# Attention steps moved into the value stage, low products turned, and the input sum one block earlier, in a one-core decoder block

## The chip, the core and the metric

The kernel runs on one core of a Trainium2 chip. The metric is device time in microseconds (us) of one execution, smaller is better. A core has a tensor engine (PE) that multiplies a loaded 128x128 block of weights with a moving matrix, a vector engine (DVE), a scalar engine (ACT), and queues through which DMA engines move data. Each engine works through its own instruction list in the order in which the kernel writes it; engines wait for one another by semaphores.

## The reference, cut to what matters

One layer of a hybrid decoder block, 256 tokens (T) by 2048 channels, all in 32-bit floats:

```
u    = rmsnorm(h, g_mix_pre)
q,k,v of 12 dilated-window heads and of 4 stick-breaking heads, and two gates = split(u @ w_in)
ya   = dilated window softmax attention (3 groups of 4 heads), groups mixed per head slot
yb   = stick-breaking attention (4 heads)
h   += rmsnorm((sigmoid(gate_a) * (ya @ w_branch_a) + sigmoid(gate_b) * (yb @ w_branch_b)) @ w_out)
h   += rmsnorm((gelu(conv(gate_ff)) * conv(value)) @ w_down)      # up projection and causal conv of width 3
h   += sigmoid(h @ w_ple_gate) * (p @ w_ple_in)
```

A head slot s (0 to 3) holds one head of each of the three window groups and one stick-breaking head. A window head needs scores q.k with a bias, a softmax over them, and the probabilities times v. The stick-breaking head needs z = q.k, l = softplus of z masked, cumulative sums of l by products with triangular ones, exp, and the result times v.

## The kernel before, in words

**Precision by splitting.** A product of two 32-bit operands is made of three products of rounded parts: high times high, high times low, low times high. Of each weight tile of 128x1024 (eight blocks of 128x128) ACT makes the rounded high part (`high`, L153) and DVE the rest (`low`, L156). The activations lie as high part (256 columns) and low part (256 columns) side by side. `mul` (L227) multiplies one block: a 512-column matmul of the high weights with both parts (L232), and a 256-column one of the low weights with the high part (L234). With `turned` the 256-column matmul goes first (L231). `mul1` and `mul_first` use three matmuls of 256 columns instead.

**Tiles and ticks.** Weight tiles come by DMA from the SP queue into five raw buffers and are split into seven pairs of high and low buffers. Every eight blocks PE reaches a new tile, and `block` calls `tick` (L181), which writes into the lists of ACT and DVE what is due: first deferred work, then the high parts of tiles some way ahead, then low parts. `defer` queues work in stages; each tick takes one new entry and runs the next stage of each entry under way (`due`, L165). Where more than two entries are waiting, the DVE part of deferred work stands before the low parts of that tick, else after them. The lookahead grows after the opening up to six tiles.

**The opening.** Seven columns (q of heads 0 to 3 and k of heads 0 to 2 of slot 0) are accumulated together, k block by k block (16 blocks), while the input arrives. At k = 14 the loop calls `flush` and `halves` (L370: the sum of squares of the input is split into two halves, DVE, ACT, DVE), at k = 15 `total` (L378: two matmuls with ones, then `rstd`, L358: the factor R on ACT and DVE). Column 7 (k of head 3) follows. The columns are taken out of PSUM by `qk_evac` (L469) in two stages: ACT copies one half of the bank, DVE adds (L286) and multiplies with R (L475); then the split into high (ACT, L484) and low (DVE, L482). Columns 0 and 1 are taken out at once, columns 2 to 7 by the ticks, one new column each: the first stage of column 2 at the first tick of column 7, that of column 6 at the third tick of the value stage.

**Slots.** For each slot come eight q and k columns (`("qk", s, c)`; slot 0 has them from the opening), then the value stage `v_units` (L507): 16 blocks kt, each with six 512-column matmuls (L517 to L519) into two banks; four weight blocks a kt, so a tick every second kt. Then the next slot's columns, and after slot 3 the gates.

**Attention steps.** `attention(s)` (L532) is a generator of eight steps; `att_step` (L624) runs one. In their order: e0 (scores of the first 128 queries, matmuls L550 on the q and k columns 0 to 2 and 4 to 6 in full precision, into the two-bank PSUM tile S; then bias, maximum, exp, sum, scaling on DVE and ACT, L556 to L560), e1 (the same for the other 128 queries, L530, on the split parts), z (L563 to L577: scores of the stick-breaking head, softplus, split), t0 and t1 (transposes of the probabilities into S, L588; copies out of it L589, L591), w (L594 to L605: cumulative sums into the PSUM tile z, exp, split), po and zo (L608 to L619: probabilities times v). S, z and po have one buffer each, so a step that writes S waits until the step before it that used S has been read out. Before, slot 0 runs two steps in its value stage, after kt = 11 and 15, the other slots four, after kt = 3, 7, 11 and 15; the rest follow one by one behind the columns of the next slot, or behind the gates. PE, DVE and ACT parts of a step stand in the engines' lists at that place.

Of the kernel before, what the change touches and what calls it, by code (L numbers as in the profile page):

```python
# [8 lines left out]
F32 = mybir.dt.float32  # L9
# [5 lines left out]
T = 256  # L15
# [18 lines left out]
LATE = 2  # L34
SETTLE = dict(even=8, turned=9)

TURNED = {("qk", 1, 1): 2, ("qk", 1, 4): 1, ("qk", 2, 1): 2, ("qk", 3, 2): 1, ("gb", 0): 2}


def _plan():  # L40
# [59 lines left out]
def hybrid_block_kernel(ctx: ExitStack, tc: tile.TileContext, gx, pT, convp, bias, masks, w, out):  # L100
# [9 lines left out]
    def f(ap):  # L110
        return ap.bitcast(F32)
# [137 lines left out]
    def mul1(ps, rhs, first, last):  # L249
# [3 lines left out]
        PE.matmul(ps, wh, rhs[:, T:], start=False, stop=False, skip_group_check=True)  # L253
        PE.matmul(ps, wl, rhs[:, :T], start=False, stop=last, skip_group_check=True)  # L254

    banks = {"of": [], "n": 0}

    def bank():
# [119 lines left out]
    def total(ps, sp):  # L378

        for n in range(2):  # L380
            PE.matmul(ps[:, :T], ones, sp[:, n * T:(n + 1) * T], start=n == 0, stop=n == 1)
        rstd(ps)
# [64 lines left out]
    for c, k, first, last in todo:  # L447
        if c == 0:
            if k == EARLY:
                at["grow"] = 0.5  # L450
                defer(*[squares2(h, (j, j + 2)) for j in range(0, KT, 4)])
            if EARLY - 2 <= k < KT - 2:
                usplit(u, k + 2, h[:, k + 2], gain(0, k + 2))
            if k == KT - 2:
                flush()
                sp = halves()
            if k == KT - 1:
                total(pat.tile([128, 2 * T], F32, name="z"), sp)
                DVE.tensor_scalar(Rq, R, 1.0 / math.sqrt(DH), None, op0=OP.mult)
        if first:  # L460
            mul_first(pss, c, u[:, k])
            c == 2 and filler(FILL)
            continue
        mul(pss[c], u[:, k], first, last)
    at["grow"] = 1
    nc.sync.dma_start(mk, masks)
    nc.sync.dma_start(cw, convp)
# [39 lines left out]
    def v_units(s):  # L507
        biases[s] = ab.tile([128, 1152], F32, name="bi")
        nc.sync.dma_start(biases[s], bias[s])
        pv = [bank() for _ in range(2)]  # L510
        assert next(plan)[0] == ("v", s)
        for kt in range(KT):
            wh, wl = block(4)
            for t in range(2):
                xh = u[:, kt, t * 128:(t + 1) * 128]
                xl = u[:, kt, T + t * 128:T + (t + 1) * 128]
                PE.matmul(pv[t], xh, wh, start=kt == 0, stop=False)  # L517
                PE.matmul(pv[t], xh, wl, start=False, stop=False)  # L518
                PE.matmul(pv[t], xl, wh, start=False, stop=kt == KT - 1)  # L519
            if kt % 4 == 3:  # L520
                yield
        V[s] = ab.tile([128, 2, 512], F32R, name="vs"), ab.tile([128, 512], F32, name="v")
        ACT.activation(V[s][0][:, 0], pv[0], AF.Copy, scale=Rc[:, 0:1])
        ACT.activation(V[s][1], pv[1], AF.Copy, scale=Rc[:, 1:2])
        DVE.scalar_tensor_tensor(V[s][0][:, 1], pv[0], Rc[:, 0:1], f(V[s][0][:, 0]), op0=OP.mult, op1=OP.subtract)
# [6 lines left out]
    def attention(s):  # L532

        (q, qs), (k, ks) = Q[s], K[s]

        def part(x, gi, a, b):

            p, _, o = split_at(x, gi)
            return [(qs if x == "q" else ks)[:, i, o + a - p:o + b - p] for i in range(2)]

        bi = biases[s]

        P = []
        for t in range(2):
            n = 128 * (t + 1)
            ps = pat.tile([128, 1024], F32, name="S")
            for gi in range(3):
                to, first = ps[:, gi * n:(gi + 1) * n], gi == 0 or (t == 1 and gi == 2)
                if t == 0:
                    PE.matmul(to, q[:, gi, :H], k[:, gi, :H], start=first, stop=True, skip_group_check=True)  # L550
                else:
                    three(to, part("q", gi, H, T), part("k", gi, 0, T), first, True)
            e = ab.tile([128, 3 * n], F32, name=f"e{t}")
            P.append(e)
            st = stats(t)
            DVE.tensor_tensor(e, ps[:, :3 * n], bi[:, 384 * t:384 * t + 3 * n], OP.add)  # L556
            DVE.tensor_reduce(st[:, 0:1], e, axis=mybir.AxisListType.X, op=OP.max, negate=True)
            ACT.activation(e, e, AF.Exp, bias=st[:, 0:1], accum_out=st[:, 1:2])
            DVE.reciprocal(st[:, 2:3], st[:, 1:2])
            DVE.tensor_scalar(e, e, st[:, 2:3], None, op0=OP.mult)  # L560
            yield

        ps = pat.tile([128, 512], F32, name="z")  # L563
        three(ps[:, :256], part("k", 3, 0, H), part("q", 3, 0, T), True, True)
        PE.matmul(ps[:, 256:384], k[:, 3, 128:], q[:, 3, 128:], start=False, stop=True, skip_group_check=True)
        z = ab.tile([128, 384], F32, name="z")
        l1 = ab.tile([128, 384], F32, name="l1")
        ACT.activation(z, ps[:, :384], AF.Copy)
        ACT.activation(l1, ps[:, :384], AF.Abs)
        ACT.activation(l1, l1, AF.Exp, scale=-1.0)  # L570
        ACT.activation(l1, l1, AF.Ln, bias=1.0)
        DVE.scalar_tensor_tensor(l1, z, 0.0, l1, op0=OP.max, op1=OP.add)
        for c in (0, 256):
            DVE.tensor_tensor(l1[:, c:c + 128], l1[:, c:c + 128], keep01, OP.mult)
        l2 = ab.tile([128, 2, 384], F32R, name="l2", tag="l2")
        ACT.activation(l2[:, 0], l1, AF.Copy)
        DVE.tensor_tensor(l2[:, 1], l1, f(l2[:, 0]), OP.subtract)  # L577
        yield

        pt = [ab.tile([128, 2, 768], F32R, name="pt0"), ab.tile([128, 384], F32, name="pt1")]  # L580
        for kb in range(2):
            ps = pat.tile([128, 1024], F32, name="S")
            w = 256 if kb == 0 else 128
            for gi in range(3):
                for t in range(kb, 2):
                    a = gi * 128 * (t + 1) + kb * 128
                    o = gi * w + (t - kb) * 128
                    PE.transpose(ps[:, o:o + 128], P[t][:, a:a + 128], ident)  # L588
            ACT.activation(pt[kb] if kb else pt[0][:, 0], ps[:, :3 * w], AF.Copy)  # L589
            if kb == 0:  # L590
                DVE.tensor_tensor(pt[0][:, 1], ps[:, :3 * w], f(pt[0][:, 0]), OP.subtract)  # L591
            yield

        ps = pat.tile([128, 512], F32, name="z")  # L594
        for c in range(2):
            PE.matmul(ps[:, :384], tri, l2[:, c], start=c == 0, stop=c == 1, skip_group_check=True)
        for c in range(2):
            PE.matmul(ps[:, 128:256], ones, l2[:, c, 256:], start=False, stop=c == 1, skip_group_check=True)
        DVE.tensor_tensor(z, z, ps[:, :384], OP.subtract)
        for c in (0, 256):  # L600
            DVE.tensor_tensor(z[:, c:c + 128], z[:, c:c + 128], neg, OP.add)
        ACT.activation(z, z, AF.Exp)
        z2 = ab.tile([128, 2, T], F32R, name="z2", tag="l2")
        ACT.activation(z2[:, 0], z[:, :T], AF.Copy)
        DVE.tensor_tensor(z2[:, 1], z[:, :T], f(z2[:, 0]), OP.subtract)  # L605
        yield

        v, v1 = V[s]  # L608
        for b in range(2):
            ps = pat.tile([128, 512], F32, name="z" if b else "po")  # L610
            heads = range(3) if b == 0 else [3]
            for gi in heads:
                x = [pt[0][:, i, gi * T:(gi + 1) * T] if b == 0 else z2[:, i] for i in range(2)]
                three(ps[:, :T], [v[:, i, gi * DH:(gi + 1) * DH] for i in range(2)], x, gi == heads[0], False)
            for gi in heads:
                x = pt[1][:, gi * H:(gi + 1) * H] if b == 0 else z[:, T:]
                PE.matmul(ps[:, H:T], v1[:, gi * DH:(gi + 1) * DH], x, start=False, stop=gi == heads[-1],
                          skip_group_check=True)
            usplit(yT, b * NS + s, ps[:, :T])  # L619
            yield  # L620
# [3 lines left out]
    def att_step():  # L624
        while stages:
            try:
                next(stages[0])
                return
            except StopIteration:
                stages.pop(0)  # L630

    for s in range(NS):
        for c in range(8 if s else 0):
            ps = mm(("qk", s, c), u, turned=TURNED.get(("qk", s, c)))
            att_step()
            qk_evac(s, c, ps)
        while stages:
            att_step()
        stages.append(attention(s))
        for c, _ in enumerate(v_units(s)):  # L640
            if c > 1 or s and c < 3:
                att_step()


    gates = {}
# [325 lines left out]
```

## Time and profile before

| | |
|---|---|
| time, median of 3 runs | 1453.83 us (1453.39 to 1454.3) |
| profiled execution, its own time | 1454.21 us |
| span of that profile | 1452.4 us |
| PE busy | 1447.1 us, 100% of the span |
| DVE busy | 1049.9 us, 72% |
| ACT busy | 826.7 us, 57% |
| granted PE clock | full in every slice of the page |

Times in the profile count from the start of the span. A row of the timeline gives start, duration, engine, line and operation, what it writes and reads, shapes, and how many in a row are merged; in square brackets stands how long the engine sat idle before it and what it waited for. Ends of matmuls are modelled: two neighbouring matmuls overlap in the rows, so the distance between starts is what one costs.

### The profile page before, as it was taken

How to read it: one execution, taken by the hardware profiler on the slowest of the kernel's cores; microseconds unless marked ns; L12 is line 12 of the kernel's file. 1: busy time of each engine (PE TensorE's matmuls, PEld its weight loads, DVE VectorE, ACT ScalarE, POOL GpSimd, SP SyncE). 2: the span in 40 equal slices, each digit the busy share in tenths (PEclk: the TensorE clock that was granted, in tenths of full speed). 3: DMA queues.
4: the chain of work that ended last, by engine and by line, in shares of the span. 5: the costliest groups of instructions: out<-in, count | busy, mean ns of one | idle time of the engine just before them, and what ended most of it. 6: DMA issues, size and time to landing. Idle time of an engine off the chain costs nothing.

```text
span 1452.4 us, 22166 instructions
## 1 busy us (share of the span) xinstructions
PE 1447.1 (100%) x8508; PEld 1281.6 (88%) x8508; DVE 1049.9 (72%) x1593; ACT 826.7 (57%) x1264; POOL 0.2 (0%) x4
## 2 busy tenths in 40 slices
PE   9999999999999999999999999999999999999998
PEld 8888888888999988998888888888888888888988
DVE  6976666666666665699965778767887678778784
ACT  6664646465545556566654556545565456567562
POOL 0000000000000000000000000000000000000000
PEclk9999999999999999999999999999999999999999
DMA  7755555566666656645766566666566666656381
GB/s 278 257 177 175 183 181 179 186 196 189 189 189 188 189 189 189 217 132 183 218 193 190 188 191 189 194 189 190 188 193 189 188 190 189 191 190 212 117 266 54
DMA packets 78442, 275.08 MB, mean 189 GB/s; under 512 B 8704, under 2 KB 11904, under 8 KB 78336
## 3 DMA queue, kind: packets, MB, share of 16 engines
q1 hardware_dynamic: 78336, 273.66, 59.5%
q8 instruction: 67, 1.10, 0.3%
q14 instruction: 39, 0.32, 0.1%
HBM read 271.53 MB, written 2.10 MB: 188 GB/s over the span
## 4 chain that ended last, share of the span: by engine, by line
PE 97%; DVE 1%; DMA 1%; ACT 1%; issue 0%; SPq 0%; DVEq 0%; ACTq 0%
PE mm L232 54%; PE mm L234 28%; PE mm L518 2%; PE mm L517 2%; PE mm L519 2%; PE mm L254 2%; PE mm L253 2%; PE mm L252 2%; DMA raw<-in_w 1%; DVE lo L156 0%; ACT hi L153 0%; PE S L530 0%; PE po L530 0%; PE S L588 0%; PE mm L242 0%
## 5 line engine op out<-in xcount | busy, mean ns | idle before, releaser
L232 PE MATMUL mm<-u,hi 128*128 128x512 f32 x2556 | 891.3, 393 | 0.0
L156 DVE TENSOR_TENSOR lo<-raw,hi 128x1024 fp32r<-128x1024 f32 (+2 forms) x512 | 614.5, 1205 | 169.0 <-ACT hi L153 161.6
L234 PE MATMUL mm<-u,lo 128*128 128x256 f32 x2533 | 709.6, 280 | 0.0
L153 ACT ACTIVATE hi<-raw 128x1024 fp32r<-128x1024 f32 (+2 forms) x512 | 531.7, 1043 | 223.5 <-PE mm L232 188.0
L232 PEld LDWEIGHTS mm<-u,hi 128*128 128x128 f32 x2556 | 477.0, 187 | 103.5
L234 PEld LDWEIGHTS mm<-u,lo 128*128 128x128 f32 x2533 | 478.7, 189 | 1.5 <-DVE lo L156 0.4
L232 PE MATMUL mm<-ft,hi 128*128 128x512 f32 x693 | 240.4, 391 | 0.0
L283 ACT ACTIVATE t<-mm 128x256 f32<-128x256 f32 x241 | 91.0, 378 | 238.8 <-PE mm L234 238.5
L234 PE MATMUL mm<-ft,lo 128*128 128x256 f32 x693 | 194.0, 280 | 0.0
L286 DVE TENSOR_TENSOR s<-mm,t 128x256 f32<-128x256 f32 x210 | 88.5, 422 | 119.4 <-ACT t L283 119.3
L232 PEld LDWEIGHTS mm<-ft,hi 128*128 128x128 f32 x693 | 129.6, 187 | 28.4
L234 PEld LDWEIGHTS mm<-ft,lo 128*128 128x128 f32 x693 | 131.0, 189 | 0.0
L232 PE MATMUL mm<-mg,hi 128*128 128x512 f32 x240 | 83.2, 391 | 0.0
L234 PE MATMUL mm<-mg,lo 128*128 128x256 f32 x239 | 66.9, 280 | 0.0
L827 ACT ACTIVATE cv<-cpad,cw 128x256 f32<-128x256 f32 x88 | 52.6, 598 | 8.1 <-DVE cpad L822 7.8
L232 PEld LDWEIGHTS mm<-mg,hi 128*128 128x128 f32 x240 | 44.8, 187 | 9.7
L517 PE MATMUL mm<-hi,u 128*128 128x512 f32 x128 | 50.7, 396 | 0.0
L518 PE MATMUL mm<-lo,u 128*128 128x512 f32 x128 | 50.0, 391 | 0.0
L519 PE MATMUL mm<-hi,u 128*128 128x512 f32 x128 | 49.9, 390 | 0.0
L234 PEld LDWEIGHTS mm<-mg,lo 128*128 128x128 f32 x239 | 45.2, 189 | 0.0
L831 DVE SCALAR_TENSOR_TENSOR cv<-cpad,cw,cv 128x256 f32<-128x256 f32 x88 | 42.6, 485 | 3.1
L830 DVE SCALAR_TENSOR_TENSOR cv<-cpad,cw,cv 128x256 f32<-128x256 f32 x88 | 42.1, 478 | 0.0
(217 smaller groups left out, 1095.2 us busy)
## 6 DMA issues: line engine op xcount, KB each, us to landing
raw<-in_w SPq DMA_DIRECT2D x506, 512.0 KB, 3.7
bi<-in_bias SPq DMA_DIRECT2D x4, 576.0 KB, 5.3
out<-t SPq DMA_DIRECT2D x16, 128.0 KB, 3.9
gh<-in_gx SPq DMA_DIRECT2D x6, 256.0 KB, 6.9
gh<-in_gx SPq DMA_DIRECT2D x3, 128.0 KB, 6.0
raw<-in_w SPq DMA_DIRECT2D x1, 384.0 KB, 4.9
raw<-in_w SPq DMA_DIRECT2D x1, 288.0 KB, 3.2
mk<-in_masks SPq DMA_DIRECT2D x1, 256.0 KB, 4.0
```

Of the source, the lines that this page charges most:

```text
L153: ACT.activation(hi[i][:, a:b], raw[i][:, a:b], AF.Copy)
L156: DVE.tensor_tensor(lo[i][:, a:b], raw[i][:, a:b], f(hi[i][:, a:b]), OP.subtract)
L232: PE.matmul(ps, wh, rhs, start=first, stop=last, skip_group_check=True)
L234: PE.matmul(ps[:, :T], wl, rhs[:, :T], start=False, stop=last, skip_group_check=True)
L283: ACT.activation(t1[0], ps[:, T:], AF.Copy)
L286: DVE.tensor_tensor(out, ps[:, :T], t1[0], OP.add)
L517: PE.matmul(pv[t], xh, wh, start=kt == 0, stop=False)
L518: PE.matmul(pv[t], xh, wl, start=False, stop=False)
L519: PE.matmul(pv[t], xl, wh, start=False, stop=kt == KT - 1)
L827: ACT.activation(y, c[:, 2:], AF.Identity, scale=cw[:, n, 2:3], bias=cw[:, n, 3:4])
L830: DVE.scalar_tensor_tensor(y, c[:, 1:T + 1], cw[:, n, 1:2], y, op0=OP.mult, op1=OP.add)
L831: DVE.scalar_tensor_tensor(y, c[:, 0:T], cw[:, n, 0:1], y, op0=OP.mult, op1=OP.add)
```

## The change

The opening calls `flush` and `halves` at k = 13 instead of 14, and `total` before column 3 of k = 14 instead of before column 0 of k = 15. At k = 4 of the opening a new function `mul3` uses three matmuls of 256 columns for a block; at k = 5 the second column is turned. In the columns 1 and 2 of the slots 1 to 3, and in the gates `("gb", 0)` and `("ga", 1)`, the third block is turned; four older entries go. The value stage yields at listed blocks: slot 0 after kt = 5, 7, 9, 13, 14, 15, the others after 1, 3, 5, 11, 13, 15, and one attention step runs at each. In the generator w comes before the transposes, and the transposes are t1, then t0. So e0, e1, z, w, t1, t0 run in the value stage and po, zo behind the next two columns (for slot 3 behind the first gate).

```diff
-TURNED = {("qk", 1, 1): 2, ("qk", 1, 4): 1, ("qk", 2, 1): 2, ("qk", 3, 2): 1, ("gb", 0): 2}
+TURNED = {("qk", s, c): 2 for s in (1, 2, 3) for c in (1, 2)} | {("gb", 0): 2, ("ga", 1): 2}
+
+STEPS = [(5, 7, 9, 13, 14, 15)] + [(1, 3, 5, 11, 13, 15)] * 3
+NARROW = 4
...
+    def mul3(ps, rhs):
+
+        wh, wl = block()
+        for out, w, x in ((ps[:, :T], wh, rhs[:, :T]), (ps[:, :T], wl, rhs[:, :T]), (ps[:, T:], wh, rhs[:, T:])):
+            PE.matmul(out, w, x, start=False, stop=False, skip_group_check=True)
...
-            if k == KT - 2:
+            if k == KT - 3:
                 flush()
                 sp = halves()
-            if k == KT - 1:
-                total(pat.tile([128, 2 * T], F32, name="z"), sp)
-                DVE.tensor_scalar(Rq, R, 1.0 / math.sqrt(DH), None, op0=OP.mult)
+        if (c, k) == (3, KT - 2):
+            total(pat.tile([128, 2 * T], F32, name="z"), sp)
+            DVE.tensor_scalar(Rq, R, 1.0 / math.sqrt(DH), None, op0=OP.mult)
         if first:
             mul_first(pss, c, u[:, k])
             c == 2 and filler(FILL)
-            continue
-        mul(pss[c], u[:, k], first, last)
+        elif k == NARROW:
+            mul3(pss[c], u[:, k])
+        else:
+            mul(pss[c], u[:, k], first, last, (c, k) == (1, NARROW + 1))
...
-            if kt % 4 == 3:
+            if kt in STEPS[s]:
                 yield
...
-        pt = [ab.tile([128, 2, 768], F32R, name="pt0"), ab.tile([128, 384], F32, name="pt1")]
-        for kb in range(2):
...
         ps = pat.tile([128, 512], F32, name="z")
         for c in range(2):
             PE.matmul(ps[:, :384], tri, l2[:, c], start=c == 0, stop=c == 1, skip_group_check=True)
...
+        pt = [ab.tile([128, 2, 768], F32R, name="pt0"), ab.tile([128, 384], F32, name="pt1")]
+        for kb in (1, 0):
...
-        for c, _ in enumerate(v_units(s)):
-            if c > 1 or s and c < 3:
-                att_step()
+        for _ in v_units(s):
+            att_step()
```

More of the change, by code (lines that the diff above doesn't have):

```diff
@@ L578, in attention @@
         yield
-        pt = [ab.tile([128, 2, 768], F32R, name="pt0"), ab.tile([128, 384], F32, name="pt1")]
-        for kb in range(2):
[L582 to L592, printed above, removed]
         ps = pat.tile([128, 512], F32, name="z")
@@ L606, in attention @@
         yield
+        pt = [ab.tile([128, 2, 768], F32R, name="pt0"), ab.tile([128, 384], F32, name="pt1")]
+        for kb in (1, 0):
+            ps = pat.tile([128, 1024], F32, name="S")
+            w = 256 if kb == 0 else 128
+            for gi in range(3):
+                for t in range(kb, 2):
+                    a = gi * 128 * (t + 1) + kb * 128
+                    o = gi * w + (t - kb) * 128
+                    PE.transpose(ps[:, o:o + 128], P[t][:, a:a + 128], ident)
+            ACT.activation(pt[kb] if kb else pt[0][:, 0], ps[:, :3 * w], AF.Copy)
+            if kb == 0:
+                DVE.tensor_tensor(pt[0][:, 1], ps[:, :3 * w], f(pt[0][:, 0]), OP.subtract)
+            yield
         v, v1 = V[s]
```

## The prediction

> **What bounds the kernel now.** I read the page first: shares of busy time, then the engines in the chain that ended last.
>
> ```profile
> span 1452.4 us, 22166 instructions
> PE 1447.1 (100%) x8508; PEld 1281.6 (88%) x8508; DVE 1049.9 (72%) x1593; ACT 826.7 (57%) x1264; POOL 0.2 (0%) x4
> PE 97%; DVE 1%; DMA 1%; ACT 1%; issue 0%; SPq 0%; DVEq 0%; ACTq 0%
> ```
>
> PE is never free. Time is won only where a matmul gets cheaper or one of PE's rare waits goes, and a wait that is put into PE's list is paid in full: no idle time follows that could give it back. The changed places lie in the first 325 us, so I compared value stages by window (columns: length, then busy time and count of PE, weight loads, DVE, ACT, POOL, then clock, DMA share, GB/s); the first row lies in slot 0's stage, the second in slot 2's.
>
> ```profile
> 54.00:77.00 23.00, 23.00 (x110) 19.27 (x109) 20.52 (x34) 14.95 (x23) 0.00 (x0) 1.00 0.83 287
> 201.00:224.00 23.00, 23.00 (x113) 19.32 (x112) 12.05 (x19) 11.44 (x18) 0.00 (x0) 1.00 0.42 141
> ```
>
> DVE is busy for 20.5 of 23 us in slot 0's stage and for 12 in slot 2's: the first still works off what the opening left. DVE's timeline shows how late it is there (last row: slot 2).
>
> ```profile
> 65.12 0.41 DVE L286 TENSOR_TENSOR s<-po,t 128x256 f32<-128x256 f32 x1
> 65.57 0.42 DVE L475 TENSOR_TENSOR k<-s,R 128x256 f32<-128x256 f32 x1
> 65.91 1.22 DVE L156 TENSOR_TENSOR lo<-raw,hi 128x1024 fp32r<-128x1024 f32 x1
> 67.05 0.42 DVE L482 TENSOR_TENSOR ks<-k,ks 128x256 fp32r<-128x256 f32 x1
> 68.18 1.22 DVE L156 TENSOR_TENSOR lo<-raw,hi 128x1024 fp32r<-128x1024 f32 x1
> 69.31 0.28 DVE L482 TENSOR_TENSOR ks<-k,ks 128x128 fp32r<-128x128 f32 x1
> 70.93 0.55 DVE L556 TENSOR_TENSOR e<-S,bi 128x384 f32<-128x384 f32 x1
> 205.96 0.56 DVE L556 TENSOR_TENSOR e<-S,bi 128x384 f32<-128x384 f32 x1 [3.28 <-PE S L550]
> ```
>
> Column 6 of the opening lies in the bank "po", so the first two rows are its first stage: k of head 2 of slot 0 is finished at 65.57 + 0.42 = 65.99. In slot 2 DVE had idled 3.28 us for step e0's scores; in slot 0 it went from low parts straight into it. PE's clock over the same stage comes from two starts, one at kt = 1 and one at kt = 6:
>
> ```profile
> 54.85 0.39 PE L517 MATMUL mm<-hi,u 128*128 128x512 f32 x1
> 61.65 0.39 PE L517 MATMUL mm<-hi,u 128*128 128x512 f32 x1
> ```
>
> One kt is (61.65 - 54.85) / 5 = 1.36 us of PE, and kt = 5 ends at 61.65. So when PE stands behind kt = 5, DVE is 4.3 us short of k of head 2.
>
> **The change part by part.**
>
> **Slot 0's six steps.** No step gains or loses an instruction, and DMAs stay where they were; only places change. Prices of the steps come from rows of the timeline, and of the chain of waits for PE (start, time, matmuls of one step with the switch behind them):
>
> ```profile
> 69.97 0.67 PE S L550 x6
> 76.13 1.07 PE S L530 x9
> 89.02 0.66 PE S L588 x6
> ```
>
> ```profile
> 208.42 2.35 DVE L156 TENSOR_TENSOR lo<-raw,hi 128x1024 fp32r<-128x1024 f32 x2
> 212.53 0.96 DVE L556 TENSOR_TENSOR e<-S,bi 128x768 f32<-128x768 f32 x1 [1.76 <-PE S L530]
> 216.31 2.35 DVE L156 TENSOR_TENSOR lo<-raw,hi 128x1024 fp32r<-128x1024 f32 x2
> 218.57 0.49 ACT L568 ACTIVATE z<-z 128x384 f32<-128x384 f32 x1 [1.13 <-PE z L565]
> 223.55 0.56 DVE L577 TENSOR_TENSOR l<-l,l 128x384 fp32r<-128x384 f32 x1 [0.59 <-ACT l L576]
> 101.76 0.56 DVE L599 TENSOR_TENSOR z<-z 128x384 f32<-128x384 f32 x1 [1.16 <-PE z L598]
> 103.89 0.43 DVE L605 TENSOR_TENSOR z<-z,z 128x256 fp32r<-128x256 f32 x1 [1.04 <-ACT z L604]
> 97.12 0.47 ACT L589 ACTIVATE pt<-S 128x384 f32<-128x384 f32 x1
> L153 ACT ACTIVATE hi<-raw 128x1024 fp32r<-128x1024 f32 (+2 forms) x512 | 531.7, 1043 | 223.5 <-PE mm L232 188.0
> ```
>
> From these: e0 holds DVE for 208.42 - 205.96 = 2.5 us, e1 for 216.31 - 212.53 = 3.8, z runs through ACT and DVE for 224.11 - 218.57 = 5.5, w for 104.32 - 101.76 = 2.6. On PE z and w take about 0.6 with the switch and t1 half of t0's 0.66 (estimates from the three rows). A low part advances DVE by 67.05 - 65.91 = 1.14; the work of the tick behind kt = 5 takes 68.18 - 65.91 = 2.3. In before's clock, list by list:
>
> *e0 (kt = 5).* PE arrives at 61.65, does heads 0 and 1 and waits from 62.1 to 66.0 for k of head 2: **3.9 us**. It leaves at 66.3. DVE is in e0 from 66.5 to 69.1, and behind it come a low part, the split of column 6 (70.6) and column 7's first stage (71.3).
>
> *e1 (kt = 7).* PE arrives at 69.0, needs that split for its last two matmuls and has it at 70.6: **0.7 us**; it leaves at 70.9. DVE is in e1 from 71.3 to 75.1, then a low part, then column 7's split, at 76.5.
>
> *z (kt = 9).* PE arrives at 73.7 and waits for column 7's split: **2.6 us**; it leaves at 76.9. The chain of z ends at 77.1 + 5.5 = 82.6.
>
> *w (kt = 13).* PE arrives at 76.9 + 0.1 + 5.4 = 82.4: **0.2 us**, out at 83.0. DVE first does the low parts of two ticks (84.9), then w, to 87.5. ACT's last copy of w ends 0.4 before (87.0).
>
> *t1 (kt = 14), t0 (kt = 15).* t1 finds S free and is out at 84.8. ACT gets to its copy only after w and the high part of that tick (1.0, last row), so S is free at 87.0 + 1.0 + 0.5 = 88.5. PE arrives for t0 at 86.1: **2.4 us**.
>
> Sum: 3.9 + 0.7 + 2.6 + 0.2 + 2.4 = **9.8 us**. Low parts themselves are not late: by 65.9 DVE has made them four tiles (11 us) ahead of PE, counted along its rows. Behind po and zo, which come a column (5.6 us) later, all is ready. Bounds: the first wait alone, 3.9, because its release needs no estimate; above, the sum.
>
> **Slots 1 to 3.** The same list for slot 2, whose stage starts at 199.63 (row below): e0's scores are there at 202.9, DVE is free for them and done at 205.8; e1 comes at 205.7 with S read out at 203.8, and z at 209.6 with column 7's split long made. z's chain starts behind e1's exp and one high part, 211.2, and ends at 216.8; w comes at 218.4, 1.6 us later. ACT has read t1 out at 223.8 and t0 comes at 224.7, 0.9 us later. The bias is the one transfer that is needed earlier:
>
> ```profile
> 197.23 0.43 SPq L509 DMA_DIRECT2D bi<-in_bias  x1
> bi<-in_bias SPq DMA_DIRECT2D x4, 576.0 KB, 5.3
> ```
>
> It lands at 202.5 and is read at 203.2. I cost these stages at nothing; the cover is 0.7 to 1.6 us thick, and if it goes, a stage costs about 1 us.
>
> **Turned blocks and the order of steps.** The same 16 blocks of a column take two lengths:
>
> ```profile
> 193.98 0.40 PE L232 MATMUL mm<-u,hi 128*128 128x512 f32 x1
> 199.63 0.40 PE L517 MATMUL mm<-hi,u 128*128 128x512 f32 x1
> 700.25 0.39 PE L232 MATMUL mm<-u,hi 128*128 128x512 f32 x1
> 705.80 0.39 PE L232 MATMUL mm<-u,hi 128*128 128x512 f32 x1
> ```
>
> 5.65 us in the last column before slot 2's stage, 5.55 in an up column: 0.10 a column. Read by such starts, PE is in the long rhythm for about 98 us between 77 and 323, behind po and zo above all; a block that is turned has brought back the short one wherever before has one. 98 / 5.65 x 0.10 = 1.7 us. A column right behind t0 that follows a value stage is already short, which is what the new order gives everywhere. Bounds 0 (the short rhythm is not reached) and 1.9; I take **-1.7**.
>
> **The opening.** PE waits there for the sum, and DVE works without a pause before it:
>
> ```profile
> 44.19 0.85 PE L381 MATMUL z<-sp,ones 128*128 128x256 f32 x2 [0.32 <-ACT sp L374]
> 46.42 0.42 DVE L363 TENSOR_SCALAR ms<-z 128x256 f32<-128x256 f32 x1 [0.69 <-ACT ln L361]
> 40.94 2.35 DVE lo L156 x2
> 43.29 0.35 DVE sq L373
> 44.65 0.39 PE z L381
> ```
>
> The last three rows are of the chain of waits: it runs over low parts, so PE cannot use a shorter rhythm (`mul3`, the turned block) before 40.9. With the halves ahead of those two low parts the sum comes at about 42.3, when PE gets to it, and the low part behind it in time (43.5, wanted at 43.9). What counts for slot 0 is DVE: it saves the 0.69 us for which it waited for ACT, and a little of PE's wait: **-0.8** (bounds 0 and -1.1). PE's own gain beyond that would only lengthen the wait for k of head 2.
>
> **Sum** against the profiled execution's own 1454.21 (span 1452.4; the median of the runs is 0.4 lower): 1454.2 + 9.8 - 1.7 - 0.8 = **1461.5 us**, 0.5% slower.
>
> **The rivals.**
>
> *Only the first wait stays* (DVE and ACT follow e0 more tightly than listed, because matmuls that wait let the low parts run ahead): 1454.2 + 3.9 - 1.7 - 0.8 = 1455.6. For it: every later wait rests on several rows in series. Against it: each of those rows is measured and DVE has no gap in them.
>
> *No wait at all: the steps are hidden.* Then only the gains count: 1454.2 - 2.5 = 1451.7, not slower. It decides from the point where k of head 2 is ready by 61.65; it would need DVE's list to be 4.3 us shorter between 44 and 66, and the change takes out 0.7.
>
> *PE's clock drops in the wait.* The start shows PE at a lower rate after idling:
>
> ```profile
> 1.04 4.42 PE L428 MATMUL z<-ones 128*128 128x128 f32 x20 [1.04 <-DVE epsb L405]
> 6.05 1.06 PE L428 MATMUL z<-ones 128*128 128x128 f32 x8
> ```
>
> 20 of these matmuls took 4.4 us there, 0.22 each; 8 later ones 1.06, 0.13. If the 3.9 us of waiting bring that back, kt = 6 and 7 take up to 2.7 us more, of which 0.7 was waiting anyway: +2.0, 1463.5. For it: the wait is the longest of the run. Against it: no row shows a drop inside the run. [...]
>
> *Slots 1 to 3 wait too*, since their cover of about 1 us is thin: 3 x 1, 1464.5.
>
> **How the numbers follow.** Forecast 0.62, only the first wait 0.12, no wait 0.08, clock 0.11, slots 1 to 3 also 0.07. What a measurement tells from no change is 0.2%, 2.9 us: 1451.3 to 1457.1 is the same. The forecast, the clock and the slots are slower, 0.80, and of the first-wait case what has one more wait in it, 0.02; the rest of that case and most of the hidden one are the same, 0.14; a hidden one with both gains at their bounds is faster, 0.04. The range leaves out most of the hidden case and the far end of the last: 1455.5 to 1465.0.
>
> **What would show it.** Right: in slot 0's stage PE stands still before the last matmuls of e0 until DVE's L475 on bank po, about 4 us; smaller waits before e1's last head, z and t0; low waits in the stages of slots 1 to 3; columns 3 to 7 at 5.55 us; PE at the sum without a wait. Wrong: DVE's first stage of column 6 before PE's kt = 6, or PE in one piece through slot 0's stage.

## The result, and the profile after

The changed kernel takes 1463.79 us (median of 4 runs, 1462.27 to 1465.49) against 1453.81 for the kernel before: ratio 1.0069, 95% interval 1.0051 to 1.0086. The forecast of 1461.5 had the direction and three quarters of the size (+7.3 forecast from the profiled execution, +10.0 measured); one of the four executions, 1465.49, lies above the forecast's range. The profiled execution took 1463.64 us at a span of 1461.8.

The page of the changed kernel, in the lines that answer to those shown of before (the chain line gives shares of the span by engine):

```profile
span 1461.8 us, 22174 instructions
PE 1449.7 (99%) x8515; PEld 1284.6 (88%) x8515; DVE 1051.4 (72%) x1593; ACT 827.2 (57%) x1264; POOL 0.2 (0%) x4
PE 95%; DVE 2%; ACT 1%; DMA 1%; issue 0%; SPq 0%; ACTq 0%; DVEq 0%
```

PE has seven more matmuls (`mul3` has three for a block where `mul` has two, once in each of seven columns) and 2.6 us more of busy time. DVE has 2% of the chain in place of 1%: PE now waits for it. The list of what PE waited for (total, times, longest) names the places (a wait of 1.0 at the start, which before has too, is left out):

```profile
PE S L561 <- DVE k L486: 4.0, 1, 4.0
PE z L541 <- DVE ks L493: 1.5, 1, 1.5
PE S L613 <- ACT pt L614: 0.8, 1, 0.8
PE z L541 <- ACT ks L495: 0.6, 1, 0.6
PE mm L513 <- DMA mk<-in_masks: 0.2, 1, 0.2
```

L561 is step e0, L541 step z (and e1), L613 the transposes, here of t0. The rows below date them: all fall into slot 0's stage. The last row is new as well: PE now reaches the transposes of R 0.2 us before the masks have landed. The timelines of DVE and of PE show the first:

```profile
64.25 0.42 DVE L295 TENSOR_TENSOR s<-po,t 128x256 f32<-128x256 f32 x1
64.70 0.43 DVE L486 TENSOR_TENSOR k<-s,R 128x256 f32<-128x256 f32 x1
66.02 0.56 DVE L567 TENSOR_TENSOR e<-S,bi 128x384 f32<-128x384 f32 x1 [0.89 <-PE S L561]
```

```profile
60.54 0.60 PE L561 MATMUL S<-k,q 128*128 128x128 f32 x4
65.18 0.80 PE L561 MATMUL S<-k,q 128*128 128x128 f32 x2 [4.04 <-DVE k L486]
65.63 0.77 PE L528 MATMUL mm<-hi,u 128*128 128x512 f32 x1
66.20 0.63 PE L529 MATMUL mm<-lo,u 128*128 128x512 f32 x1
66.63 0.63 PE L530 MATMUL mm<-hi,u 128*128 128x512 f32 x1
70.47 0.39 PE L530 MATMUL mm<-hi,u 128*128 128x512 f32 x1
77.22 0.56 PE L541 MATMUL z<-qs,ks 128*128 128x256 f32 x1 [1.49 <-DVE ks L493]
89.44 0.87 PE L613 MATMUL S<-mk,e 128*128 128x128 f32 x6 [0.83 <-ACT pt L614]
```

PE does heads 0 and 1 and stands until DVE has finished k of head 2, at 65.13. Something else is in these rows: behind the wait two matmuls of 512 columns start 66.20 - 65.63 = 0.57 and then 0.43 us apart, where 0.227 is usual, until 70.47 (0.227 is a sixth of the 1.36 us of a kt). The windows (length, busy PE, weight loads, DVE, ACT, POOL, then the granted clock) say why:

```profile
60.20:63.60 3.40, 0.94 (x7) 0.67 (x5) 3.40 (x4) 1.63 (x3) 0.00 (x0) 1.00 0.89 324
65.50:70.40 4.90, 4.90 (x13) 3.91 (x13) 3.51 (x8) 2.23 (x5) 0.00 (x0) 0.50 0.65 250
70.40:77.20 6.80, 4.78 (x25) 3.63 (x23) 4.45 (x7) 2.37 (x5) 0.00 (x0) 1.00 0.26 77
77.20:80.60 3.40, 3.38 (x10) 2.80 (x11) 0.00 (x0) 2.29 (x4) 0.00 (x0) 0.51 0.41 154
```

The clock was halved twice, from within the wait of e0 on and behind that of z. In the other slots' stages PE waits for nothing, and the opening goes as forecast: the sum's two matmuls come at 42.13 without a wait (before: 44.19, behind one).

```profile
42.13 0.42 PE L390 MATMUL z<-sp,ones 128*128 128x256 f32 x2
52.24 0.48 PE L528 MATMUL mm<-hi,u 128*128 128x512 f32 x1
```

The value stage of slot 0 starts at 52.24 in place of 53.13 (first row, of before). It ends where the next column starts, and the last two rows give the same two places of slot 2, with the same six steps:

```profile
53.13 0.48 PE L517 MATMUL mm<-hi,u 128*128 128x512 f32 x1
```

```profile
90.07 0.48 PE L235 MATMUL mm<-u,hi 128*128 128x512 f32 x1
209.51 0.39 PE L528 MATMUL mm<-hi,u 128*128 128x512 f32 x1
235.31 0.47 PE L235 MATMUL mm<-u,hi 128*128 128x512 f32 x1
```

Slot 0's stage takes 90.07 - 52.24 = 37.83 us and slot 2's 25.80: 12.0 us are lost there. The span is only 9.4 longer; 0.9 comes back in the opening, and the rest of the kernel is 1.7 us shorter. So three things were to be told apart: the waits of slot 0 against everything else, one late operand against DVE's list as a whole, and the waits against the clock.

### The profile page after: what moved, and what is told of

The parts are those of the page before. It is cut to its first block, busy times and chain, and to the rows that moved or that the text cites. A ratio compares the mean times of both kernels' runs of the same rounds, so it can differ in the third digit from the quotient of the medians.

```text
span 1461.8 us, 22174 instructions
## 1 busy us (share of the span) xinstructions
PE 1449.7 (99%) x8515; PEld 1284.6 (88%) x8515; DVE 1051.4 (72%) x1593; ACT 827.2 (57%) x1264; POOL 0.2 (0%) x4
## 4 chain that ended last, share of the span: by engine, by line
PE 95%; DVE 2%; ACT 1%; DMA 1%; issue 0%; SPq 0%; ACTq 0%; DVEq 0%
PE mm L235 54%; PE mm L237 28%; PE mm L257 2%; PE mm L256 2%; PE mm L255 2%; PE mm L528 2%; PE mm L529 2%; PE mm L530 2%; DVE lo L159 1%; DMA raw<-in_w 1%; ACT hi L156 1%; PE S L541 0%; PE po L541 0%; PE mm L245 0%; PE mm L250 0%
## 5 line engine op out<-in xcount | busy, mean ns | idle before, releaser
L528 PE MATMUL mm<-hi,u 128*128 128x512 f32 x128 | 53.0, 414 | 0.0
L530 PE MATMUL mm<-hi,u 128*128 128x512 f32 x128 | 51.3, 401 | 0.0
```

## The experiments

The medians of the kernel before lie between 1453.81 and 1454.09 in the different groups of runs, so a difference between two kernels of different groups is good to about 0.3 us.

### Slot 0 alone, undone: late0

```diff
-STEPS = [(5, 7, 9, 13, 14, 15)] + [(1, 3, 5, 11, 13, 15)] * 3
+STEPS = [(11, 15)] + [(1, 3, 5, 11, 13, 15)] * 3
```

> The changed kernel with slot 0's steps e0 and e1 back behind kt = 11 and 15 (the other six follow behind the columns of slot 1); all else as changed. If the loss lies in slot 0's value stage alone, only the gains are left: about 0.9 us of the opening and 1.4 to 1.7 us of the rhythm off 1453.8, so 1451.2 to 1451.7. If slots 1 to 3 or the new order of the steps lose too, it stays at 1453 or more.

1452.78 us (median of 11 runs, 1452.12 to 1453.68) against 1454.02 of before in the same group of runs: ratio 0.9991, interval 0.9982 to 1.0. All of the loss is gone, 11.0 us against the changed kernel's 1463.79; so slots 1 to 3 with their six early steps and the new order of the steps cost nothing that shows. The gain that is left, 1.2, is about half of what was expected; the spans of single profiles say 1450.6 against 1452.4, 1.8. Part of what is missing lies in slot 1: from the start of slot 0's stage to that of slot 1's PE takes 73.25 us here, from slot 1's to slot 2's 72.63; six steps stand behind slot 1's columns, and only two of these columns have a turned block (turn5 below has more). PE's list of waits has, beside the one at the start, a small one:

```profile
PE mm L237 <- DVE lo L159: 0.2, 1, 0.2
```

### The input sum as before: late0_sum

On top of late0:

```diff
-            if k == KT - 3:
+            if k == KT - 2:
                 flush()
                 sp = halves()
-        if (c, k) == (3, KT - 2):
+        if (c, k) == (0, KT - 1):
             total(pat.tile([128, 2 * T], F32, name="z"), sp)
```

> As late0, with the input sum back at k = 14 and its matmuls back at k = 15. If the earlier sum is worth what PE and DVE save there, this is 0.8 to 0.9 us slower than late0 (1452.3). If that wait is only passed on to the next one, the two are equal.

1453.52 (11 runs, 1452.62 to 1454.45), 0.7 over late0; the ranges overlap, so the size is rough. The profile has PE's wait back, in the list of waits:

```profile
PE z L390 <- ACT sp L383: 0.4, 1, 0.4
```

By the runs the earlier sum is worth about what was forecast (0.8). In the profiles slot 0's stage starts at 53.85 here and at 52.43 in late0, 1.4 apart, but the execution profiled here is 0.6 over its median. The wait is not passed on in full: late0 has 0.2 for a low part instead.

### No block turned: late0_noturn

On top of late0:

```diff
-TURNED = {("qk", s, c): 2 for s in (1, 2, 3) for c in (1, 2)} | {("gb", 0): 2, ("ga", 1): 2}
+TURNED = {}
-NARROW = 4
+NARROW = -9
```

> As late0, but no column, gate or opening block is turned and the opening has no block of three narrow matmuls; what was turned before the change is not turned either. If a turned block is what brings the short rhythm back, the columns behind po and zo run at 5.65 us in place of 5.55: 1.5 to 2.3 us slower than late0 (1453.3). If the rhythm comes back by itself, the two are equal.

1454.48 (11 runs, 1453.96 to 1455.63), 1.7 over late0 and the ranges do not touch. From the start of slot 2's value stage to that of slot 3 the timelines of PE give 72.60 us in late0 (first two rows) and 73.28 without turned blocks (last two):

```profile
198.31 0.39 PE L528 MATMUL mm<-hi,u 128*128 128x512 f32 x1
270.91 0.39 PE L528 MATMUL mm<-hi,u 128*128 128x512 f32 x1
```

```profile
198.82 0.40 PE L528 MATMUL mm<-hi,u 128*128 128x512 f32 x1
272.10 0.40 PE L528 MATMUL mm<-hi,u 128*128 128x512 f32 x1
```

That is 0.68 a slot, the size of seven columns at 0.10: it fits with the long rhythm lasting, without a turned block, through all columns behind po. Behind one turned block the short one is there: in the changed kernel's profile, after the block turned at 176.91, 16 blocks take 5.54 us (177.62 to 183.16). Why PE falls into the long rhythm no run here shows. In the opening this does not show: without `mul3` and the turned block slot 0's stage starts at 52.17, in late0, with both, at 52.43.

### Three steps in slot 0's stage, later: mid0

```diff
-STEPS = [(5, 7, 9, 13, 14, 15)] + [(1, 3, 5, 11, 13, 15)] * 3
+STEPS = [(9, 11, 13)] + [(1, 3, 5, 11, 13, 15)] * 3
```

> The changed kernel with e0, e1 and z of slot 0 behind kt = 9, 11 and 13. If what costs is that PE asks before DVE has got to column 6, nothing is left of it here (k of head 2 is there at 65.1 and PE comes at 66.2, and the following reads are 0.5 to 2 us ahead of PE): within 0.3 us of late0. If every step inside slot 0's stage is paid because DVE is behind, three steps cost 3 us or more: 1454.5.

1452.75 (11 runs, 1451.92 to 1453.6), ratio to before 0.999 (0.9981 to 0.9999), equal to late0. The timelines of DVE and PE show how near it is:

```profile
64.71 0.43 DVE L486 TENSOR_TENSOR k<-s,R 128x256 f32<-128x256 f32 x1
69.08 0.55 DVE L567 TENSOR_TENSOR e<-S,bi 128x384 f32<-128x384 f32 x1
```

```profile
65.97 0.83 PE L561 MATMUL S<-k,q 128*128 128x128 f32 x6
```

PE comes 0.8 us after k of head 2 is there. DVE reads the scores only 2.5 us later and is done at 69.63, and e1, which follows two kt behind and writes S, starts at 69.68: between the matmuls of the value stage it takes 1.67 us, in late0 1.30. These 0.4 us stand in no list of waits, since an idle time counts from the modelled end of the matmul before it. A step inside the stage is not what costs; a step whose operand stands too far down DVE's list is.

### The first step alone: e0only

```diff
-STEPS = [(5, 7, 9, 13, 14, 15)] + [(1, 3, 5, 11, 13, 15)] * 3
+STEPS = [(5, 11, 13)] + [(1, 3, 5, 11, 13, 15)] * 3
```

> The changed kernel with slot 0's e0 behind kt = 5 as changed, e1 and z behind kt = 11 and 13, the other steps behind the columns of slot 1. Theory: the 4.2 us of the first wait and what the clock adds (0 to 2 us) remain over the kernel without waits (1452.8): 1457.0 to 1459.0. If the first wait is what makes all the rest late, most of the 11 us stays: 1461 or more.

1458.31 (6 runs, 1457.54 to 1460.22): 5.6 us over mid0, with a wait of 4.0 and a stretch of halved clock (0.51 from 63.5 to 70.4) that begins within it. PE's list of waits and the windows:

```profile
PE S L561 <- DVE k L486: 4.0, 1, 4.0
```

```profile
63.50:66.90 3.40, 1.50 (x5) 1.31 (x6) 2.45 (x6) 1.08 (x2) 0.00 (x0) 0.51 0.99 374
66.90:70.40 3.50, 3.50 (x10) 2.73 (x9) 2.69 (x6) 2.23 (x5) 0.00 (x0) 0.51 0.36 144
```

So the first wait is half of the loss of 11; the other half, with its share of the clock, comes from the five steps that follow it closely. In the changed kernel's profile z and t0 wait, each for an operand or a buffer of its own that DVE or ACT had not got to.

### The one late operand taken away: khead

```diff
-                    PE.matmul(to, q[:, gi, :H], k[:, gi, :H], start=first, stop=True, skip_group_check=True)
+                    PE.matmul(to, q[:, gi, :H], k[:, min(gi, 1) if s == 0 else gi, :H], start=first, stop=True, skip_group_check=True)
```

> The changed kernel, but step e0 of slot 0 reads k of head 1 in place of k of head 2 (the result of that head is another one), so PE does not wait there. If what is late is DVE's list as a whole, the wait only moves on: PE stands at e1 for the reading of S (65.7) and for the split of column 6 (69.1), and only the 0.9 us that DVE waited for e0's scores and part of the clock are saved: 1461 to 1462. If the wait for that one operand is the loss, 4 us and the clock go: 1458 or less.

The kernel leaves out k of head 2 in this one step. 1461.34 (5 runs, 1460.92 to 1462.06): 2.4 us less than the changed kernel, not 4 and more. PE's list of waits has no L561 any more, and in its place (1.0 at the start and 0.6 for low parts aside):

```profile
PE S L613 <- ACT pt L614: 1.8, 1, 1.8
PE S L541 <- DVE e L567: 1.6, 1, 1.6
PE S L541 <- DVE ks L493: 1.4, 1, 1.4
PE z L541 <- DVE ks L493: 1.1, 1, 1.1
PE S L541 <- ACT ks L495: 0.7, 1, 0.7
```

```profile
69.00:72.40 3.40, 3.26 (x9) 2.68 (x10) 2.76 (x5) 0.45 (x1) 0.00 (x0) 0.50 0.52 154
```

The last fence is a window of the same kernel: its granted clock was 0.50 in these 3.4 us. The wait moved to e1 (L541 into S): 1.6 until DVE had read S, 2.1 more for the split of column 6 (0.7 for ACT's part, 1.4 for DVE's). Removing the operand at which DVE's list shows only shows the next row of it.

### PE kept busy through the wait: fill, fill17

```diff
             for gi in range(3):
+                if s == 0 and t == 0 and gi == 2:
+                    busy = bank()
+                    for _ in range(17):
+                        PE.matmul(busy[:, :128], f(ones), f(ones), start=True, stop=True)
                 to, first = ps[:, gi * n:(gi + 1) * n], gi == 0 or (t == 1 and gi == 2)
```

A first kernel, fill, had 36 in place of 17.

> The changed kernel, with 36 matmuls of ones (128 columns, 0.11 us each, 4.0 us in all, into a bank that nobody reads) put into step e0 of slot 0 ahead of head 2, so that PE works through the time in which it would wait for k of head 2. If the halved clock costs time of its own beside the wait, it goes: DVE gets e0's scores 0.5 us earlier and e1's 1.2 us earlier, the time falls by 1.5 to 2 us to about 1462, and runs differ less. If DVE's list sets the pace whatever PE's clock, it stays at 1463.8.

1466.23 (4 runs, 1465.49 to 1466.83), slower than the changed kernel by 2.4. It was mis-sized, and the timeline of PE says by how much:

```profile
61.31 8.20 PE L562 MATMUL mm<-ones 128*128 128x128 f32 x72
```

36 instructions of the kernel stand as 72 in the profile and took 8.0 us; PE passed e0 at 69.6 and not at 65.2. It tells nothing on the price of the clock. It tells something else: PE was so late that DVE had finished k of head 2 and then stood still for 4.3 us until it got e0's scores (timeline of DVE):

```profile
69.77 0.56 DVE L571 TENSOR_TENSOR e<-S,bi 128x384 f32<-128x384 f32 x1 [4.31 <-PE S L565]
```

Even so e1 waits 0.5, z 0.7 + 1.5 and t0 1.8, the same as with 17 below. These waits are thus not a backlog of the opening: the splits of the columns 6 and 7 stand in DVE's list behind the work of the step before, so DVE cannot use its idle time for them, and ACT's copy for t0 stands behind its work for w. With 17, beside the changed kernel:

> As fill, with 17 matmuls of ones in place of 36: one full-precision matmul of 128 columns showed up as two records of 0.11 us, so 36 of them took 8.0 us and themselves held PE until 69.4. 17 take 3.8 us and end where k of head 2 is ready. If the halved clock costs time of its own, this is 1.5 to 2 us faster than the changed kernel run beside it; if DVE's list sets the pace whatever PE's clock, they are equal.

> The changed kernel as it is, beside fill17 on the same chip: 1462 to 1465.5, as before, its executions 3 us apart.

1462.02 (5 runs, 1461.63 to 1462.32). The changed kernel beside it: 1463.55 (5 runs, 1462.09 to 1464.57), ratio to before 1.0065 (1.0051 to 1.0078). The two ranges overlap in 0.2 us; the medians differ by 1.5, and the spread falls from 2.5 to 0.7. In the profiled execution with 17 (1462.03) the clock is full throughout; the other four have a mean clock of 0.998 or 0.999, so it may have fallen in some of them too, but their times are no longer. These are the waits without the clock in them (timeline of PE, with the start of the stage and of the next column; one window with its clock last but two):

```profile
52.21 0.48 PE L528 MATMUL mm<-hi,u 128*128 128x512 f32 x1
61.21 3.96 PE L562 MATMUL mm<-ones 128*128 128x128 f32 x34
65.42 0.49 PE L565 MATMUL S<-k,q 128*128 128x128 f32 x2 [0.25 <-DVE k L486]
70.01 0.50 PE L541 MATMUL S<-ks,qs 128*128 128x256 f32 x2 [0.50 <-DVE ks L493]
73.92 0.50 PE L541 MATMUL z<-qs,ks 128*128 128x256 f32 x2 [0.66 <-ACT ks L495]
75.91 0.39 PE L541 MATMUL z<-qs,ks 128*128 128x256 f32 x1 [1.49 <-DVE ks L493]
87.73 0.88 PE L617 MATMUL S<-mk,e 128*128 128x128 f32 x6 [1.82 <-ACT pt L618]
88.37 0.48 PE L235 MATMUL mm<-u,hi 128*128 128x512 f32 x1
```

```profile
52.00:92.00 40.00, 35.24 (x186) 28.97 (x187) 29.48 (x50) 26.17 (x41) 0.00 (x0) 1.00 0.56 186
```

The stage takes 88.37 - 52.21 = 36.16 us, 10.4 more than slot 2's 25.79 in this kernel. The profiled execution of the changed kernel beside it (again, 1462.09) waits 3.9 for e0 and has its clock halved once between 60 and 81 us, from about 65.0 to 68.4 (the granted clock is 0.91 from 60 to 66 and 1.00 from 71 to 81; between them the window over the end of it):

```profile
66.00:71.00 5.00, 5.00 (x23) 4.22 (x22) 3.82 (x9) 2.23 (x5) 0.00 (x0) 0.77 0.45 143
```

Its stage takes 36.47 us, 0.3 more than that of fill17, and that of the first profile of the changed kernel, with 10.2 us at half clock, 37.83, 1.7 more. From the start of the stage to k of head 2 DVE took 12.8, 12.9 and, in fill17, 13.2 us; allowing for that, the halved clock cost 0.7 and 1.9 us. Part of what a slower PE loses it would have waited anyway.

### The gains alone: turn5

mid0, with blocks turned behind each of the five steps that lie behind slot 1's columns there:

```diff
-TURNED = {("qk", s, c): 2 for s in (1, 2, 3) for c in (1, 2)} | {("gb", 0): 2, ("ga", 1): 2}
+TURNED = {("qk", s, c): 2 for s in (1, 2, 3) for c in range(1, 6 if s == 1 else 3)} | {("gb", 0): 2, ("ga", 1): 2}
```

> Slot 0's e0, e1 and z behind kt = 9, 11 and 13, and the third block turned in the columns 1 to 5 of slot 1 in place of 1 and 2, since five steps lie behind its columns here. If a turned block brings the short rhythm back behind every step, slot 1's columns lose the 0.5 us that they still have over it: 1452.3, the fastest of all. If the rhythm behind these steps is short already, a turned block lengthens it: 1452.8 or more.

1452.11 (11 runs, 1451.38 to 1453.74) against 1454.09 of before: ratio 0.9988 (0.9979 to 0.9997), the lowest median of all, though the ranges of turn5 and mid0 overlap. Its profile has no wait of PE behind the start, and 2.0 of the forecast gains of 2.5 us are left in the runs. From slot 0's stage to slot 1's its profile takes 72.92 us (mid0: 73.48).

## Why the prediction was right, point by point

**What bounds the kernel: right.** PE was never free, so slot 0's waits were paid in full: taking them away (late0, mid0) gives back all of it (11.0 us each).

**k of head 2: right.** Forecast was a wait of 3.9 us from column 6's place in DVE's list; the profile has 4.04, released by exactly that row.

**The chain behind it: right in kind and in size.** An idle time in square brackets counts from the modelled end of the matmul before it and comes out short. By starts, a step costs the distance between the matmuls of the value stage on its two sides, less the same distance in slot 2: for e0 in fill17 5.41 - 0.81. At full clock (fill17, profiled execution), in us:

| step | forecast | idle in the rows | by starts |
|---|---|---|---|
| e0 | 3.9 | 3.96 of added matmuls, 0.25 | 4.60 |
| e1 | 0.7 | 0.50 | 0.76 |
| z | 2.6 | 0.66 + 1.49 | 2.68 |
| w | 0.2 | none | 0.24 |
| t1 | 0 | none | 0 |
| t0 | 2.4 | 1.82 | 2.05 |
| sum | 9.8 | 8.7 | 10.3 |

The sum of 9.8 is met within 0.5: e0 has 0.7 more and t0 0.35 less, and the time at which k of head 2 is ready differs by 0.4 between executions. As times, fill17 lies 1462.02 - 1452.75 = 9.3 us over mid0, whose own steps still lose some (e1 0.4). The rival of a first wait alone falls: e0only has just that and is 5.6 over mid0, clock included, half of the changed kernel's 11. In the changed kernel's own profile e1 does not wait: at half clock PE comes to it too late (at 70.69, with the split of column 6 done at 70.03).

**Slots 1 to 3 at nothing: right.** No wait stands in their stages, all three take 25.80 us, and with slot 0 undone no loss shows. The cover of 0.7 to 1.6 us held.

**The gains: right together, 2.5 forecast.** In the changed kernel's profile slot 0's stage starts 0.9 us earlier (0.8 forecast), and what is left of the span beside that stage is 1.7 shorter (1.7 forecast). The turned blocks are worth 1.7 against none at all (late0_noturn), but the kernel before had some already. Versions that leave steps of slot 0 behind slot 1's columns lose a part: by runs 1.2 remains against before in late0, 1.3 in mid0 and 2.0 in turn5.

**The clock: the step that failed.** I gave it as a rival with a chance of 0.11 and a price of 2.0, and the forecast's sum has nothing for it. It happened in the profiles of the changed kernel (both), of e0only and of khead. The runs fit: e0only took 1457.5 and 1458.0 us at a mean clock of 0.999, 1458.3 twice at 0.998, 1459.0 and 1460.2 at 0.997. A value of 0.999 alone says little, since runs of the kernel before have it too. The price is 1.5 by the medians of fill17 and the changed kernel, whose ranges overlap a little, and 1.9 and 0.7 by the stages of the two profiles of the changed kernel. The forecast's 1461.5 was the time at full clock; the profiled execution of fill17, which had it, took 1462.03. What failed is the chance: the 0.11 was my estimate, which no run shows, and no row of before tells after what wait the clock falls. The rows at the start, from which I took the price, show a lower rate but not a lower clock: before's windows give 1.00 for 0 to 4, 4 to 5 and 5 to 7 us. In the changed kernel the clock was granted at half from 63.6 on (0.50 from 63.6 to 70.4), 2.5 us after the wait of e0 began (60.54 + 0.60), with PE busy for 0.94 of the 3.4 us before. The time still fell into the range because the range took in this rival (1463.5) and that of the slots 1 to 3 (1464.5).

**Rhythm before 40.9 in the opening:** no gain shows. The opening's blocks were undone together with the turned blocks (late0_noturn), and slot 0's stage then starts at 52.17, no later than in late0 (52.43); a run that changes them alone was not made.

## What to carry to other kernels

When a step is moved earlier on the busiest engine, look up the row that makes its last operand, and read how late the engine that makes it runs at that place, not how busy it is on the mean: DVE was 72% busy over the span and more than 4 us behind in this one stage. Moving a group of steps in a row repeats the question for each of them, and taking away the operand that shows the wait only moves it to the next (khead won 2.4 us, the wait was 4.0). An operand that stands in a list behind the step before it comes late even when that engine has idle time (fill: DVE idle for 4.3 us, PE's waits in e1 and z still 0.5 to 1.5). Place a step where the row that releases it has already ended (here kt = 9 in place of 5) and keep the moves that cost nothing.

## What the runs showed of the hardware that was not expected

PE's clock fell though PE had worked for part of the time just before: in the 3.4 us ahead of the first drop (as long as the second stretch at half clock, 77.2 to 80.6) PE was busy for 0.94 us, and ahead of the second drop for 1.38 of 3.42 (ends of matmuls are modelled).

```profile
73.86:77.28 3.42, 1.38 (x7) 0.71 (x5) 2.17 (x5) 2.37 (x5) 0.00 (x0) 1.00 0.00 0
```

The second drop stands behind waits of 0.6 + 1.5 us in z. Waits of 0.7 + 1.5 there in fill17 and of 0.6 + 1.5 in again brought no drop in their profiles (granted clock 1.00 from 52 to 92 us and from 71 to 81), so how long PE waits does not decide alone. What else decides was not shown; executions of the changed kernel are 2.5 to 3.2 us apart and those of fill17 0.7. And a full-precision matmul of 128 columns by 128 stands as two records and takes twice 0.11 us (fill: 72 records for 36 matmuls, 8.0 us).
